# A one-core decoder step in split float32: where weights and x start in SBUF, the order of the last stores, and the place of the low-rank products

## The chip, the cores and the metric

The kernel runs on one core of one Trainium2 chip. The metric is the device time of one execution, in microseconds; the median of several runs is compared. The profile is one execution taken by the hardware profiler.

## The reference

One inference step of a decoder layer for two groups of tokens, 256 prompt tokens and 32 sample tokens (8 sequences of 4), with a width of 2048:

```python
def trunk(x, ...):
    x = x + 0.5 * rmsnorm(swiglu(rmsnorm(x, g[0]), ffn1_w_in, ffn1_w_out), g[1])
    m, sg, sh = hybrid_mixer(rmsnorm(x, g[2]), mix_w_in, gla_w_gate_up, ..., mix_w_out, s_gla, s_hgrn)
    x = x + rmsnorm(m, g[3])
    x = x + 0.5 * rmsnorm(swiglu(rmsnorm(x, g[4]), ffn2_w_in, ffn2_w_out), g[5])
    return x, sg, sh

def swiglu(x, w_in, w_out):                 # w_in 2048 x 11264, w_out 5632 x 2048
    gate, up = jnp.split(x @ w_in, 2, axis=-1)
    return (jax.nn.silu(gate) * up) @ w_out

def hybrid_mixer(h, w_in, ...):
    q, k, v, a_lr, r, hq, hf, hi, hg = jnp.split(h @ w_in, ...)
    log_alpha = jax.nn.log_sigmoid(a_lr @ gla_w_up + gla_b) / 16.0    # a_lr has 16 columns
    ...   # two gated linear recurrences (4 GLA heads, 8 HGRN2 heads), norm per head, gates
    return merged @ w_out, s_gla_new, s_hgrn_new
```

All tensors are float32, and the outputs are y for both groups and the new states.

## The kernel before

**Tiles.** All 288 tokens (T) are the columns of every product. x is held as 16 tiles of 128 x 288, one for each 128 of the 2048 features (k = 0 to 15). Each float32 operand of a large product is split into a high part (float32r) and a low part (the rest): xh[k] and xl[k] for x, hh and hl for the hidden layer, wh and wl for weights. A product is then three TensorE instructions: wh with xh (L591), wh with xl (L592), wl with xh (L593), all into one accumulator. The weights are the stationary operand (128 x 128), x the moving one (128 x 288).

**Weights.** `Weights` streams them in 672 units of 128 x 1024: two k steps of 512 columns each. SyncE's queue loads a unit into one of three `raw` buffers (L64), `pieces` splits it: ScalarE copies raw to wh (L96), VectorE subtracts to get wl (L97). There are four buffers of wh and wl, and near the borders between layers a wider pool (`begin_extra`) holds two more for some units. `ahead` keeps the split in front of TensorE.

**Blocks.** `block` makes 512 output columns: four accumulators (f = 0 to 3), for every k the four column blocks with three products each, so 12 products a k step; the last unit of a block goes by f first (`tail`), so that accumulators finish one after another. After each k, `tick(k)` emits other work. The order of instructions on each engine is made by a scheduler from the program and from `issue_after`.

**Order of the work.** Feed-forward 1: 11 chunks of gate and up blocks (16 k steps each) and output blocks (four k steps, eight at the end); the mixer; feed-forward 2 likewise. In the mixer, block v0 carries in its ticks the row mean of x (`tick1`, with `rstd` at k = 11 that gives rt), `scale_lr` at k = 8 and `a_lr` at k = 12. `a_lr` makes the 16 low-rank columns (L1445), adds up four partial sums (L1447, L1449), multiplies by rt (L1450) and splits the result and the weights for the decay product zp (L1463). The block after v0 is qk1.

**The end.** In the last output block each finished tile y[k] is added (L755), squared (L422 or L420) and scaled to z (L764); TensorE turns the last four to token order (L730, L737). `finish` makes the mean over features (L432, L160, L437: rc) and then adds z times rc to x (L809), eight prompt pieces of 128 x 512 and one sample piece zS, each followed by its store on SyncE's queue (L822, four stores L815 for zS).

**Addresses.** As the allocator places them, the bytes at which operands start in a partition, modulo 256, are: x tiles (1152 bytes each) 64 for even k and 192 for odd k; wh and wl 192 throughout (units of 4096 bytes, column blocks of 512), except for 28 units in the wider pool at 224; hidden tiles 0 and 128 in turn.

Of the kernel before, what the change touches and what calls it, by code (L numbers as in the profile page):

```python
# [30 lines left out]

RAW_BUFS = 3
HL_BUFS = 4
SCAN_LAG = 4
X_EARLY = 12


class Weights:
# [46 lines left out]
    def pieces(self, n):  # L85

        i = self.split
        raw = self.raws.pop(i)
        pool = self.extra if i in self.extra_units else self.hlp
        h = pool.tile([P, 1024], F32R, name=f"wh{i}", tag="wh")  # L90
        l = pool.tile([P, 1024], F32R, name=f"wl{i}", tag="wl")
        self.parts[i] = (h, l)
        self.split += 1
        for c in range(0, 1024, 1024 // n):
            c = slice(c, c + 1024 // n)
            i1 = self.nc.scalar.activation(h[:, c], raw[:, c], AF.Copy).ins  # L96
            i2 = self.nc.vector.tensor_tensor(l[:, c], raw[:, c], h[:, c].bitcast(F32), op=ALU.subtract).ins  # L97
            self.recent = i1, i2
            yield i1, i2

# [26 lines left out]
def trunk_kernel(ctx, tc, x_prompt, x_sample, state_gla, state_hgrn, norm_gains, f1_in, f1_out, f2_in, f2_out,  # L127
# [378 lines left out]
    class Fill:  # L506
# [3 lines left out]
        def __init__(self, pool, name, gains, gnext, some, ahead):  # L510
            self.gnext, self.name, self.some, self.ahead = gnext, name, some, ahead

            self.gains = pool.tile([P, EARLY], F32, name=f"{name}g")
            V.tensor_tensor(self.gains, gains[:, 0:EARLY], prm[:, gnext * KT:gnext * KT + EARLY], op=ALU.mult)
            self.tiles = [[[pool.tile([P, T], F32R, name=f"{name}{n}{p}{k}") for p in "hl"] for k in range(EARLY)]
                          for n in "xy"]

        def old(self):
            for k in range(EARLY):
# [62 lines left out]
    def block(name, nk, rhs, evac, width=512, tick=None, tail=1, hold=False, most=99, fill=None, late=0):  # L582

        nf, per = width // P, 1024 // width
        nu = nk // per
        ps = [mmtile(f"{name}_{f}") for f in range(nf)]
        ws = [W.next() for _ in range(EARLY // per)] if fill else []

        def mm3(dst, w, f, k, parts, start, stop):
            c = (k % per) * width + f * P  # L590
            yield lambda: PE.matmul(dst, w[0][:, c:c + P], parts[0], start=start, stop=False)  # L591
            yield lambda: PE.matmul(dst, w[0][:, c:c + P], parts[1], start=False, stop=False)  # L592
            yield lambda: PE.matmul(dst, w[1][:, c:c + P], parts[0], start=False, stop=stop)  # L593
# [48 lines left out]
    def ffn(tag, gcol, gnext, pn, before, fill=None):  # L642
# [3 lines left out]
        with ExitStack() as pools:  # L646
# [93 lines left out]
            def do_out(c, n):  # L740
# [8 lines left out]
                for o in range(4):  # L749
                    def ev(f, ps):  # L750
                        k = 4 * o + f
                        if c == 0:
                            S.activation(y[k], ps, AF.Copy)
                        else:
                            V.tensor_tensor(y[k], ps, y[k], op=ALU.add)  # L755
                        if end:
                            sq = sq_add(y[k], k, 0, KT - 2, KT - 1)
                            if k >= KT - 1:
                                lasts.append(sq)
                            if not final:  # L760
                                border[0].fill.new(k)
                            else:
# [20 lines left out]
            if final:  # L783
                zt, xt = final_tiles[0:2]

                def rest():
                    by_token(zs[2], KT - 2, *zt)
                    by_token(zs[3], KT - 1, *zt)
                    samples(zs, zt[1])

                finish(lasts[0][0], rest, zt, xt)
                return None
        return post_norm(gcol, gnext, lasts, f"post{tag}", border[0].fill), border[0]

    def finish(last, rest, zt, xt):

        (zT, zS), (xT, xS) = zt, xt
        ms = auxtile("postf")
        rc, _ = mean_cols(ms, [[sq[:, t * P:(t + 1) * P] for t in range(2)] for sq in (acc, last)], 0, 2, True)
        four = []  # L800
        for sq in (acc, last):
            r = sqp.tile([P, 4, TS], F32, name="sq4", tag="pn")
            G.tensor_copy(r, sq[:, TP:T].unsqueeze(1).broadcast_to([P, 4, TS]))
            four.append([r.rearrange("p a b -> p (a b)")])
        rest()
        rcs, _ = mean_cols(ms, four, 2, 3, False)

        def add(o, z, x, t):
            V.scalar_tensor_tensor(o, z, rc[:, t:t + 1] if t < 2 else rcs, x, op0=ALU.mult, op1=ALU.add)  # L809

        for s in range(4):
            if s == 3:
                add(zS, zS, xS, 2)
                for q in range(4):
                    nc.sync.dma_start(y_sample[:, :, q * 512:(q + 1) * 512].rearrange("b t c -> (b t) c"),  # L815
                                      zS[q * TS:(q + 1) * TS, :])

            o = (hlp if s else rawp).tile([P, 2, 512], F32, name=f"o{s}", tag="wh" if s else "raw")
            for t in range(2):
                k = slice(4 * s, 4 * s + 4)  # L820
                add(o[:, t].rearrange("p (k c) -> p k c", c=P), zT[:, k, t], xT[:, k, t], t)
                nc.sync.dma_start(y_prompt[0, t * P:(t + 1) * P, s * 512:(s + 1) * 512], o[:, t])  # L822


    def mixer(pn, border):
        with ExitStack() as mx:
# [614 lines left out]
            def a_lr():  # L1441
# [46 lines left out]
            for g in range(2):  # L1488
# [155 lines left out]
```

## Time and profile before

| | before |
|---|---|
| median of 3 runs (lowest to highest) | 2248.1 us (2247.73 to 2248.68) |
| the profiled execution: time, span | 2247.12 us, 2245.3 us |
| granted TensorE clock | 0.998 |
| TensorE, weight loads | 2233.0 us busy (99%), 2218.3 us |
| VectorE, ScalarE, GpSimd | 1386.3 us (62%), 1022.8 us (46%), 171.2 us (8%) |
| loads from memory | 167 GB/s over the span |

PE is TensorE's matmul, PEld its weight load, DVE VectorE, ACT ScalarE, POOL GpSimd, SP SyncE, and a q behind the name is the queue of an engine. A timeline row gives start and duration in us, engine, line, operation and tiles (output, then inputs), shape and count; in brackets the idle time before it. A group's row gives line, engine, operation, tiles, shapes and count, then busy us and the mean ns of one, then the idle time of the engine before it and who ended it. Rows of a window give, for each engine, the busy us and the number of instructions in the order PE, PEld, DVE, ACT, POOL, then the granted clock, the share of the DMA engines and GB/s.

### The profile page before, as it was taken

How to read it: one execution, taken by the hardware profiler on the slowest of the kernel's cores; microseconds unless marked ns; L12 is line 12 of the kernel's file. 1: busy time of each engine (PE TensorE's matmuls, PEld its weight loads, DVE VectorE, ACT ScalarE, POOL GpSimd, SP SyncE). 2: the span in 40 equal slices, each digit the busy share in tenths (PEclk: the TensorE clock that was granted, in tenths of full speed). 3: DMA queues.
4: the chain of work that ended last, by engine and by line, in shares of the span. 5: the costliest groups of instructions: out<-in, count | busy, mean ns of one | idle time of the engine just before them, and what ended most of it. 6: DMA issues, size and time to landing. Idle time of an engine off the chain costs nothing.

```text
span 2245.3 us, 43325 instructions
## 1 busy us (share of the span) xinstructions
PE 2233.0 (99%) x17832; PEld 2218.3 (99%) x17832; DVE 1386.3 (62%) x2252; ACT 1022.8 (46%) x1556; POOL 171.2 (8%) x311
## 2 busy tenths in 40 slices
PE   9999999999999999999999999999999999999998
PEld 9999999999999999999999999999999999999998
DVE  7545545554555568888888755944555465545646
ACT  6443333333334345555676654544333333333344
POOL 2000000000000001333000000530000000000005
PEclk9999999999999999999999999999999999999999
DMA  7555555555555554667565554665555555555555
GB/s 223 171 169 162 167 168 162 168 167 163 169 165 182 170 164 141 194 197 213 174 172 169 178 184 130 195 186 164 165 169 164 165 169 164 165 169 163 166 166 152
DMA packets 226758, 384.28 MB, mean 171 GB/s; under 512 B 21106, under 2 KB 60544, under 8 KB 226560
## 3 DMA queue, kind: packets, MB, share of 16 engines
q1 hardware_dynamic: 213968, 365.15, 51.8%
q0 software_dynamic: 10416, 16.18, 2.7%
q8 instruction: 140, 2.29, 0.4%
q10 hardware_dynamic: 2176, 0.18, 0.1%
q14 instruction: 58, 0.48, 0.1%
HBM read 363.75 MB, written 11.80 MB: 167 GB/s over the span
## 4 chain that ended last, share of the span: by engine, by line
PE 99%; DVE 0%; POOL 0%; ACT 0%; issue 0%; DVEq 0%; POOLq 0%
PE gate L591 10%; PE gate L593 10%; PE gate L592 10%; PE out L592 8%; PE up L593 8%; PE up L591 8%; PE up L592 8%; PE out L593 8%; PE out L591 8%; PE hfq L591 2%; PE hfq L593 2%; PE hfq L592 2%; PE mo L593 2%; PE mo L591 2%; PE mo L592 2%; PE hi L591 1%
## 5 line engine op out<-in xcount | busy, mean ns | idle before, releaser
L97 DVE TENSOR_TENSOR wl<-raw,wh 128x1024 fp32r<-128x1024 f32 (+1 forms) x676 | 821.8, 1217 | 616.7 <-ACT wh L96 612.8
L96 ACT ACTIVATE wh<-raw 128x1024 fp32r<-128x1024 f32 (+1 forms) x676 | 711.5, 1054 | 1018.8 <-PE gate L592 308.8
L591 PE MATMUL gate<-xh,wh 128*128 128x288 f32 x1660 | 489.4, 296 | 0.0
L593 PE MATMUL gate<-xh,wl 128*128 128x288 f32 x1660 | 487.7, 295 | 0.0
L592 PE MATMUL gate<-xl,wh 128*128 128x288 f32 x1660 | 485.7, 295 | 0.0
L592 PE MATMUL out<-hl,wh 128*128 128x288 f32 x1408 | 416.1, 296 | 0.0
L593 PE MATMUL up<-xh,wl 128*128 128x288 f32 x1408 | 415.6, 295 | 0.0
L593 PE MATMUL out<-hh,wl 128*128 128x288 f32 x1408 | 415.3, 295 | 0.0
L592 PE MATMUL up<-xl,wh 128*128 128x288 f32 x1408 | 415.1, 295 | 0.0
L591 PE MATMUL up<-xh,wh 128*128 128x288 f32 x1408 | 415.0, 295 | 0.0
L591 PE MATMUL out<-hh,wh 128*128 128x288 f32 x1408 | 414.1, 294 | 0.0
L591 PEld LDWEIGHTS gate<-xh,wh 128*128 128x128 f32 x1660 | 311.3, 188 | 0.9 <-DVE z L1533 0.2
L593 PEld LDWEIGHTS gate<-xh,wl 128*128 128x128 f32 x1660 | 311.4, 188 | 0.2 <-DVE wl L97 0.2
L592 PEld LDWEIGHTS gate<-xl,wh 128*128 128x128 f32 x1660 | 310.7, 188 | 0.3
L593 PEld LDWEIGHTS out<-hh,wl 128*128 128x128 f32 x1408 | 265.0, 188 | 0.0
L591 PEld LDWEIGHTS out<-hh,wh 128*128 128x128 f32 x1408 | 264.9, 188 | 0.0
L592 PEld LDWEIGHTS out<-hl,wh 128*128 128x128 f32 x1408 | 264.7, 188 | 0.0
L593 PEld LDWEIGHTS up<-xh,wl 128*128 128x128 f32 x1408 | 264.6, 188 | 0.0
L592 PEld LDWEIGHTS up<-xl,wh 128*128 128x128 f32 x1408 | 264.4, 188 | 0.0
L591 PEld LDWEIGHTS up<-xh,wh 128*128 128x128 f32 x1408 | 264.3, 188 | 0.0
L755 DVE TENSOR_TENSOR y<-out,y 128x288 f32<-128x288 f32 x288 | 121.3, 453 | 101.3 <-PE out L593 98.3
L720 POOL DMA_DIRECT2D zT<-b x40 | 23.2, 586 | 721.7 <-issue 721.7
(396 smaller groups left out, 2573.2 us busy)
## 6 DMA issues: line engine op xcount, KB each, us to landing
raw<-in_ffn_w_in_dram SPq DMA_DIRECT2D x350, 512.0 KB, 3.5
raw<-in_ffn_w_out_dram SPq DMA_DIRECT2D x176, 512.0 KB, 3.6
raw<-in_mix_w_in_dram SPq DMA_DIRECT2D x64, 512.0 KB, 4.0
raw<-in_mix_w_in_dram SPq DMA_DIRECT2D x96, 256.0 KB, 3.2
raw<-in_mix_w_out_dram SPq DMA_DIRECT2D x32, 512.0 KB, 3.7
out_dram<-s POOLq DMA_DIRECT2D x32, 256.0 KB, 2.8
s<-in_state_gla_dram SPq DMA_DIRECT2D x16, 256.0 KB, 4.7
s<-in_state_hgrn_dram SPq DMA_DIRECT2D x16, 256.0 KB, 5.3
```

Source lines behind the costliest of these rows:

```text
L96: i1 = self.nc.scalar.activation(h[:, c], raw[:, c], AF.Copy).ins
L97: i2 = self.nc.vector.tensor_tensor(l[:, c], raw[:, c], h[:, c].bitcast(F32), op=ALU.subtract).ins
L591: yield lambda: PE.matmul(dst, w[0][:, c:c + P], parts[0], start=start, stop=False)
L592: yield lambda: PE.matmul(dst, w[0][:, c:c + P], parts[1], start=False, stop=False)
L593: yield lambda: PE.matmul(dst, w[1][:, c:c + P], parts[0], start=False, stop=stop)
L720: queues[n % len(queues)].dma_start(dst[q * TS:(q + 1) * TS, 4 * g:4 * g + 4, :, cols].rearrange("p k t c -> p (k t) c"), b32[rows, q])
L755: V.tensor_tensor(y[k], ps, y[k], op=ALU.add)
```

## The change

Three edits. (1) A weight unit is [2, 544] instead of [1024], that is, its second k step starts 2176 bytes behind the first, and each buffer is 4352 bytes; a 32-column tile `cols`, a 40-column tile ahead of the wider pool and the order of the border's tiles shift what lies behind. As the allocator places them, the starts modulo 256 are then 64 for even and 192 for odd k of every unit, x as before. (2) In `finish`, the last tile is added and squared by halves of its tokens, each half has a mean and a square root of its own, and the sample's mean and the last tiles' turning come behind; the prompt pieces 0 to 2 go first for the first 128 tokens, then for the second (the scheduler mixes the two somewhat); the sample's four stores go to ScalarE's queue, and the two last prompt pieces come behind the sample's add. (3) `a_lr` ends after the partial sums and runs at k = 10; what needs rt is in `lr_parts`, at k = 12.

Distance is the start of the weights for the next product less the start of the operand that streams, modulo 256. Of the 16,034 pairs of successive large products have, in the built programs:

| distance | 0 | 64 | 128 | 192 | 32, 96, 160, 224 |
|---|---|---|---|---|---|
| before | 5664 | 1992 | 5671 | 1992 | 715 |
| after | 10482 | 842 | 1330 | 3380 | 0 |

```diff
+HALF = 512 + 32
...
-        h = pool.tile([P, 1024], F32R, name=f"wh{i}", tag="wh")
-        l = pool.tile([P, 1024], F32R, name=f"wl{i}", tag="wl")
+        h = pool.tile([P, 2, HALF], F32R, name=f"wh{i}", tag="wh")
+        l = pool.tile([P, 2, HALF], F32R, name=f"wl{i}", tag="wl")
...
-            i1 = self.nc.scalar.activation(h[:, c], raw[:, c], AF.Copy).ins
-            i2 = self.nc.vector.tensor_tensor(l[:, c], raw[:, c], h[:, c].bitcast(F32), op=ALU.subtract).ins
+            i1 = self.nc.scalar.activation(h[:, a, c], raw[:, a, c], AF.Copy).ins
+            i2 = self.nc.vector.tensor_tensor(l[:, a, c], raw[:, a, c], h[:, a, c].bitcast(F32), op=ALU.subtract).ins
...
+    cols = xpool.tile([P, 32], F32, name="cols")
...
-            c = (k % per) * width + f * P
-            yield lambda: PE.matmul(dst, w[0][:, c:c + P], parts[0], start=start, stop=False)
+            a, c = k % per, slice(f * P, f * P + P)
+            yield lambda: PE.matmul(dst, w[0][:, a, c], parts[0], start=start, stop=False)
...
+                        elif final and end and k == KT - 1:
+                            sq = sqp.tile([P, T], F32, name="sq", tag="sq")
+                            with ExitStack() as es:
+                                for r in (slice(0, P), slice(P, T)):
+                                    V.tensor_tensor(y[k][:, r], ps[:, r], y[k][:, r], op=ALU.add)
+                                    ins = V.tensor_tensor(sq[:, r], y[k][:, r], y[k][:, r], op=ALU.mult).ins
+                                    es.enter_context(tc.issue_after(ins))
+                            lasts.append((sq, None))
...
+        mss = [mmtile(f"postf{t}") for t in range(2)]
+        rc = [cols[:, 8 * t:8 * t + 1] for t in range(3)]
...
+        for sq in (acc, last):
+            for t in range(2):
+                total(sq[:, t * P:(t + 1) * P], t, sq is acc, sq is last)
+        scale(0)
+        scale(1)
...
+        for i in range(2):
+            tot = total(four[i], 2, False, i == 1)
+        behind = scale(2)
+        rest(behind, tot)
...
+        for t in range(2):
+            for s in range(3):
+                prompt(s, t)
+        add(zS, zS, xS, 2)
+        for q in range(4):
+            S.dma_start(y_sample[:, :, q * 512:(q + 1) * 512].rearrange("b t c -> (b t) c"), zS[q * TS:(q + 1) * TS, :])
+        for t in range(2):
+            prompt(3, t)
...
+            def lr_parts():
                 V.tensor_tensor(alr32[0:16, :], alr32[0:16, :], rt[0:16, :], op=ALU.mult)
...
-                          tick=lambda k: (pn.tick1(k), scale_lr() if k == 8 else a_lr() if k == 12 else None))
+                          tick=lambda k: (pn.tick1(k), scale_lr() if k == 8 else a_lr() if k == 10 else lr_parts() if k == 12 else None))
...
+            top = self.pools.enter_context(tc.tile_pool(name=f"top{gnext}", bufs=1, side="right"))
+            top.tile([P, 40], F32, name=f"gap{gnext}")
```

More of the change, by code (lines that the diff above doesn't have):

```diff
@@ L511, in __init__ @@
             self.gnext, self.name, self.some, self.ahead = gnext, name, some, ahead
-            self.gains = pool.tile([P, EARLY], F32, name=f"{name}g")
+            tiles = [[[pool.tile([P, T], F32R, name=f"{name}{n}{p}{k}") for k in range(EARLY)] for p in "hl"] for n in "xy"]
+            self.tiles = [list(zip(*hl)) for hl in tiles]
+            self.gains = pool.tile([P, 64], F32, name=f"{name}g")[:, 0:EARLY]
             V.tensor_tensor(self.gains, gains[:, 0:EARLY], prm[:, gnext * KT:gnext * KT + EARLY], op=ALU.mult)
-            self.tiles = [[[pool.tile([P, T], F32R, name=f"{name}{n}{p}{k}") for p in "hl"] for k in range(EARLY)]
-                          for n in "xy"]
         def old(self):
@@ L753, in ev @@
                             S.activation(y[k], ps, AF.Copy)
+                        elif final and end and k == KT - 1:
[6 more added lines that the diff above has]
+                            lasts.append((sq, None))
                         else:
                             V.tensor_tensor(y[k], ps, y[k], op=ALU.add)
-                        if end:
+                        if end and not (final and k == KT - 1):
                             sq = sq_add(y[k], k, 0, KT - 2, KT - 1)
@@ L759, in ev @@
                                 lasts.append(sq)
+                        if end:
                             if not final:
                                 border[0].fill.new(k)
-                            else:
+                            elif k < KT - 1:
                                 z = fp.tile([P, T], F32, name="z", tag="z", bufs=4)
@@ L784, in ffn, with rest @@
                 zt, xt = final_tiles[0:2]
-                def rest():
-                    by_token(zs[2], KT - 2, *zt)
+                def rest(ins, tot):
+                    with tc.issue_after(tot):
+                        for i in (1, 2):
+                            by_token(zs[i], KT - 4 + i, *zt)
+                    z = fp.tile([P, T], F32, name="z", tag="z", bufs=4)
+                    with tc.issue_after(ins):
+                        S.activation(z, y[KT - 1], AF.Copy, scale=gcol(KT - 1))
+                    zs.append(z)
                     by_token(zs[3], KT - 1, *zt)
@@ L797, in finish, with total, scale @@
         (zT, zS), (xT, xS) = zt, xt
-        ms = auxtile("postf")
-        rc, _ = mean_cols(ms, [[sq[:, t * P:(t + 1) * P] for t in range(2)] for sq in (acc, last)], 0, 2, True)
+        mss = [mmtile(f"postf{t}") for t in range(2)]
+        rc = [cols[:, 8 * t:8 * t + 1] for t in range(3)]
+        def total(cols, t, start, stop):
+            return PE.matmul(mss[t % 2][:, t:t + 1], cols, onesD[:, 0:1], start=start, stop=stop, skip_group_check=True).ins
+        def scale(t):
+            ins = act(rc[t], mss[t % 2][:, t:t + 1], AF.Sqrt, bias=epst)
+            V.reciprocal(rc[t], rc[t])
+            return ins
+        for sq in (acc, last):
[3 more added lines that the diff above has]
+        scale(1)
         four = []
@@ L803, in finish, with prompt @@
             G.tensor_copy(r, sq[:, TP:T].unsqueeze(1).broadcast_to([P, 4, TS]))
-            four.append([r.rearrange("p a b -> p (a b)")])
-        rest()
-        rcs, _ = mean_cols(ms, four, 2, 3, False)
-        def add(o, z, x, t):
[L809 to L822, printed above, removed]
+            four.append(r.rearrange("p a b -> p (a b)"))
+        for i in range(2):
+            tot = total(four[i], 2, False, i == 1)
+        behind = scale(2)
+        rest(behind, tot)
+        def add(o, z, x, t):
+            V.scalar_tensor_tensor(o, z, rc[t], x, op0=ALU.mult, op1=ALU.add)
+        outs = [(hlp if s else rawp).tile([P, 2, 512], F32, name=f"o{s}", tag="wh" if s else "raw") for s in range(4)]
+        def prompt(s, t):
+            k, o = slice(4 * s, 4 * s + 4), outs[s][:, t]
+            add(o.rearrange("p (k c) -> p k c", c=P), zT[:, k, t], xT[:, k, t], t)
+            nc.sync.dma_start(y_prompt[0, t * P:(t + 1) * P, s * 512:(s + 1) * 512], o)
+        for t in range(2):
[6 more added lines that the diff above has]
+            prompt(3, t)
     def mixer(pn, border):
```

11 lines of the change are left out of this document (7 added, 4 removed).

## The prediction

> **What bounds the kernel now.** I read the page first (busy times, then the chain that ended last), then TensorE's own rows in order of time, then the last 14 us of every engine, and last the neighbourhood of the low-rank products.
>
> ```profile
> span 2245.3 us, 43325 instructions
> ...
> PE 2233.0 (99%) x17832; PEld 2218.3 (99%) x17832; DVE 1386.3 (62%) x2252; ACT 1022.8 (46%) x1556; POOL 171.2 (8%) x311
> ...
> PE 99%; DVE 0%; POOL 0%; ACT 0%; issue 0%; DVEq 0%; POOLq 0%
> ```
>
> TensorE is busy for all but 12.3 us of the span, and the chain of waits is TensorE for 99%. So only two things can move the time: the pitch at which TensorE starts one product after another, and the stretch after the last product. "Busy" does not tell the pitch, because a product's row lasts 0.29 us while the next one starts 0.13 us later. The starts do. One k step is 12 products (four column blocks of three products), all with the same x tile k, xh or xl. These are the first rows of three successive steps, k = 0, 1 and 2, of the gate block of chunk 3 of the first feed-forward:
>
> ```profile
> 214.00 0.30 PE L591 MATMUL gate<-xh,wh 128*128 128x288 f32 x1
> ...
> 215.60 0.29 PE L591 MATMUL gate<-xh,wh 128*128 128x288 f32 x1
> ...
> 217.18 0.30 PE L591 MATMUL gate<-xh,wh 128*128 128x288 f32 x1
> ```
>
> Step 0 takes 1.60 us, step 1 takes 1.58 us. The same instructions and shapes, and no wait in either. The alternation goes on through the block. What differs is the address: x starts at 64 for even k and at 192 for odd k (modulo 256), the weights at 192 for both. Call distance the start of the weights being loaded for the next product less the start of the operand now streaming, modulo 256: it is 128 in the slow steps and 0 in the fast ones. Is it the address or the parity of k? The kernel has its own control. 28 of the 672 weight units lie in the wider pool, at 224. There k even has distance 160 and k odd has 32. Steps 8 and 9 of a gate block that uses such a unit, with the start of step 10:
>
> ```profile
> 761.02 0.30 PE L591 MATMUL gate<-xh,wh 128*128 128x288 f32 x1
> ...
> 762.60 0.30 PE L591 MATMUL gate<-xh,wh 128*128 128x288 f32 x1
> ...
> 764.20 0.29 PE L591 MATMUL gate<-xh,wh 128*128 128x288 f32 x1
> ```
>
> Now the even step takes 1.58 and the odd one 1.60: the parity is turned round by the address alone. The hidden tiles of the output products lie at 0 and 128; their two steps have distances 192 and 64:
>
> ```profile
> 271.27 0.29 PE L591 MATMUL out<-hh,wh 128*128 128x288 f32 x1
> ...
> 272.85 0.29 PE L591 MATMUL out<-hh,wh 128*128 128x288 f32 x1
> ...
> 274.45 0.30 PE L591 MATMUL out<-hh,wh 128*128 128x288 f32 x1
> ```
>
> 1.58 at 192, 1.60 at 64. So distances 0, 160 and 192 are fast, 32, 64 and 128 slow, by about 20 ns in a step.
>
> **The change, the layout.** It gives the two halves of a weight unit starts 128 apart, so that x of either parity meets weights at distance 0, and the hidden tiles meet distance 192. Of the 16,034 pairs of successive products 5,664 have distance 0 before and 10,482 after; 192 goes from 1,992 to 3,380; 128 falls from 5,671 to 1,330, which are the hand-overs from one k to the next, once in 12. A hand-over at 128 costs 20 ns / 12 = 1.7 ns more than one at 0.
>
> Steps that stream x in the ordinary order: 496 units of two steps, less the last unit of each of 62 blocks (their order is by column block), some 866 steps. Before they cost (1.60 + 1.58)/2 = 1.590 us, after 1.580 + 0.002 = 1.582: 8 ns x 866 = 6.9 us. Output products of the feed-forwards: 176 units, 82 of them last units, so 188 ordinary steps, 1.590 to 1.582 as well: 1.5 us. In the last units of blocks k changes after every third product, so that one pair in three has distance 128 (or 64) where it was every second; I count nothing for them. That is 8.4 us. The starts are printed to 10 ns; the same sum over all 16,034 pairs of the trace (the quoted rows are nine of them), grouped by distance modulo 512 and weighted with the counts after, gives 7.1. I take **7.7 us** off, midway, with 3.5 (only the half that is seen today, below) and 10.5 (all steps at the best of the trace, the last units too) as ends.
>
> A page speaks against this. The Trainium skill, "SBUF — State Buffer", section "Who interferes with whom", gives TensorE two independent read ports, one for the moving operand and one for the weights, and states that "PE and ACT never wait on anyone"; by that the layout is worth nothing. The rows above do not agree: 1.58 and 1.60 us for the same step, by address.
>
> The splits (L96, L97) now write two runs of 512 with a gap. Strided shapes of the same engine bound that:
>
> ```profile
> L424 DVE TENSOR_TENSOR acc<-acc,sq 128x288 f32<-128x288 f32 x87 | 39.3, 452 | 7.6 <-ACT sq L420 4.8
> ```
> ```profile
> L1104 DVE TENSOR_TENSOR Q<-Q,F 128x256 f32<-128x256 f32 x30 | 12.7, 422 | 4.4 <-PE sc L1044 4.0 <-ACT R L1119 0.3
> ```
>
> L424 is flat; the 256 elements of L1104 lie in pieces such as 2 x 32 x 4. 288 against 256 elements differ by 30 ns, 0.94 ns an element, so the strides cost nothing that shows. Zero, and at most one more fixed part of 452 - 288 x 0.94 = 181 ns a split, which the idle time of VectorE hides (second fence of the rivals). The x tiles, loads and number of splits stay.
>
> **The end.** VectorE's rows after the last product, and the last stores on SyncE's queue:
>
> ```profile
> 2231.97 0.46 DVE L755 TENSOR_TENSOR y<-out,y 128x288 f32<-128x288 f32 x1 [0.36 <-PE out L593]
> 2232.46 0.46 DVE L422 TENSOR_TENSOR sq<-y 128x288 f32<-128x288 f32 x1
> 2233.91 0.17 DVE L437 RECIPROCAL rc<-rc 128x2 f32<-128x2 f32 x1 [0.99 <-ACT rc L160]
> 2234.11 2.74 DVE L809 SCALAR_TENSOR_TENSOR o<-zT,rc,xT 128x512 f32<-128x512 f32 x4
> 2236.77 0.16 DVE L437 RECIPROCAL rc<-rc 128x1 f32<-128x1 f32 x1
> 2236.84 1.40 DVE L809 SCALAR_TENSOR_TENSOR o<-zT,rc,xT 128x512 f32<-128x512 f32 x2
> 2238.15 0.75 DVE L809 SCALAR_TENSOR_TENSOR zS<-zS,rc,xS 128x512 f32<-128x512 f32 x1
> 2238.81 1.41 DVE L809 SCALAR_TENSOR_TENSOR o<-zT,rc,xT 128x512 f32<-128x512 f32 x2
> ```
> ```profile
> 2238.93 2.12 SPq L815 DMA_DIRECT2D out_dram<-zS  x4
> 2241.14 0.88 SPq L822 DMA_DIRECT2D out_dram<-o  x2
> ```
>
> Before: from the first row to the first add of the output is 2.14 us; nine adds and a reciprocal take until 2240.22. The last two stores stand behind the sample's four on one queue, so the last goes at 2241.14 + 0.44 = 2241.6, 1.4 us after its data. After: a first half of 128 tokens takes 0.30 instead of 0.46 in each of the two operations (452 less 160 x 0.94), so its total can start 0.3 earlier; the transposes of the tile before no longer stand ahead of the totals on TensorE, nor the scaling of the last tile ahead of the square root on ScalarE. I let the adds start 0.5 us earlier and add 0.07 for the third reciprocal (pitch from 2236.77 to 2236.84). They end at 2239.8, and the last prompt store goes at once: 1.8 us sooner than 2241.6. The sample's add ends after seven adds and two reciprocals, at 2233.6 + 7 x 0.685 + 0.14 = 2238.55 (0.685 is 2.74/4). Its four stores now follow on ScalarE's queue:
>
> ```profile
> L865 ACTq DMA_DIRECT2D araw<-in_mix_w_in_dram x1: 398/398/398, 60.4 to 60.4; - x1
> ```
> ```profile
> L815 SPq DMA_DIRECT2D out_dram<-zS x4: 314/326/359, 2238.9 to 2240.7; - x4
> ```
>
> An issue there took 398 ns against 326 on SyncE, so four take 2.12 + 4 x 0.07 = 2.4 us and the last starts near 2240.4: still 1.2 us sooner than 2241.6. ScalarE has nothing left to do behind them. I take the end **1.5 us** shorter, between 0.4 (the stores on ScalarE's queue issue at half the rate) and 2.2. ScalarE's own work (three square roots first, then z, three copies of zT and zS) is done before the seventh add.
>
> **Low-rank products two steps up.** TensorE does the same work in another order:
>
> ```profile
> 901.10 2.13 PE L1445 MATMUL a_lr<-x,y 128*16 128x288 f32 x32
> ```
> ```profile
> 902.21 0.46 DVE L471 SCALAR_TENSOR_TENSOR rt<-rsls,rslsg 128x288 f32<-128x288 f32 x1
> ```
> ```profile
> 908.68 1.19 DVE L979 TENSOR_TENSOR y<-v,rt 128x288 f32<-128x288 f32 x3
> ```
> ```profile
> 909.19 0.40 PE L591 MATMUL qk<-xh,wh 128*128 128x288 f32 x1 [0.18 <-DVE y L979]
> ```
>
> Before, the three sums of the low-rank result stand between rt and the evictions of v on VectorE, and TensorE idles 0.18 us at 909.19 waiting for one of those evictions. After, the sums come before rt, but the 2.13 us of products now stand ahead of the row-mean products of pre2, so rt comes some 2 us later, and the evictions of v and the decay's products that need it with it. Against that stand the sums that no longer delay the evictions and, in the built order, eight products of qk1_0 (about 1 us) that TensorE does before it needs the first of them. I take 0, between -0.2 (the small wait gone) and +1.0.
>
> **Sum.** 7.7 + 1.5 + 0 = 9.2 us. The profiled execution took 2247.12 us with a span of 2245.3; it becomes 2237.9. The median of the runs is 1.0 us above it, 2248.1: **2238.9 us**.
>
> **Rivals.**
>
> Half of the layout only. The pairs seen today have weights at 192 (or 224). If weights at 64, which half of the steps now use, run like the average of today, half of the 7.7 us comes: 2242.8. For: no row has weights at 64. Against: at 224 the relation moved with the address, it did not vanish. Chance 0.12.
>
> No layout effect. If the pitch follows something that goes with the buffers and not with the distance, the sum is the end alone: 2246.6. Against it stand the fast even steps at 761.02. This is where the page's two ports would lead too. Chance 0.10.
>
> The low-rank order makes rt late. The late rt holds the evictions of v, qk1's accumulators and then zp; if all 2.13 us reach TensorE, they come back: 2241.0. Chance 0.05.
>
> Slower: the split with a gap binds VectorE in the mixer.
>
> ```profile
> 945.00:1262.00 317.00, 317.00 (x3250) 306.70 (x3249) 265.87 (x590) 202.71 (x455) 52.94 (x84) 1.00 0.63 185
> ```
> ```profile
> L97 DVE TENSOR_TENSOR wl<-raw,wh 128x1024 fp32r<-128x1024 f32 x78 | 95.2, 1221 | 16.2 <-ACT wh L96 14.3 <-PE tp_k L926 1.0 <-PE hms L1346 0.3
> ```
>
> VectorE has 317 - 265.9 = 51.1 us idle there over 78 splits, 0.66 us each, so it decides from a split of 1.88 us instead of 1.22. If each run of 512 cost as much as a whole row does (2.44), 78 x 1.22 - 51 = 44 us would come on top: 2283. Against it stands L1104. Chance 0.04.
>
> **How the numbers follow.** The forecast holds 0.69, with a range of its own from 2235.5 (10.5 + 2.2) to 2242.8. A comparison of this kernel tells 0.2%, 4.5 us, from no change. Faster by more: forecast, the half (2242.8 is 5.3 us off), the late rt: 0.85, a little of each falling short. Same: 0.11. Slower: 0.04. The range runs from 2234.8, just below the forecast's own low end, to 2244.5, past the half.
>
> **What would show it.** Right: even and odd steps of a gate block both at 1.58 us; the last store about 1.5 us nearer to the last product; L97 still near 1.22 us. Wrong: an alternation of 1.58 and 1.60 that remains, or moves to the other parity; a wait of qk over 1 us near 909; ScalarE's stores as the last to land.

## The result and the profile after

The changed kernel takes **2237.2 us** (median of six runs, 2236.34 to 2238.57) against 2248.1 us: 11.0 us or 0.5% faster, ratio 0.9952, 95% interval [0.9939, 0.9965]. The prediction was 2238.9 us, with a range from 2234.8 to 2244.5. The profiled execution took 2238.57 us, the longest of the six, with a span of 2236.7 us.

The page of the changed kernel, in the lines that answer to those of before:

```profile
span 2236.7 us, 43325 instructions
...
PE 2223.8 (99%) x17832; PEld 2207.8 (99%) x17832; DVE 1385.8 (62%) x2255; ACT 1021.9 (46%) x1557; POOL 169.5 (8%) x311
...
DVE 0%; DVEq 0%
```

The same number of products, and TensorE still busy for all but 12.9 us. The chain is no help this time: it ends at an add behind the last product and does not reach TensorE. The pitch must again be read from the starts. TensorE's timeline of the changed kernel, the first rows of steps k = 0 to 3 of the same gate block as in the prediction (chunk 3 of the first feed-forward):

```profile
213.57 0.29 PE L596 MATMUL gate<-xh,wh 128*128 128x288 f32 x1
...
215.15 0.29 PE L596 MATMUL gate<-xh,wh 128*128 128x288 f32 x1
...
216.72 0.29 PE L596 MATMUL gate<-xh,wh 128*128 128x288 f32 x1
...
218.30 0.30 PE L596 MATMUL gate<-xh,wh 128*128 128x288 f32 x1
```

1.58, 1.57, 1.58: the alternation of 1.60 and 1.58 is gone. But the up block that follows, with the same x at the same distance 0, runs otherwise (the first rows of its steps 0 to 2):

```profile
238.82 0.29 PE L596 MATMUL up<-xh,wh 128*128 128x288 f32 x1
...
240.41 0.30 PE L596 MATMUL up<-xh,wh 128*128 128x288 f32 x1
...
242.00 0.29 PE L596 MATMUL up<-xh,wh 128*128 128x288 f32 x1
```

1.59 in each step, even and odd. It stays so to the end of that block. So distance 0 gives not one pitch but two, 1.577 or 1.590 us a step, and a feed-forward block keeps the one it has to its end. Call them the fast and the slow phase. Over half of all x steps run in the slow one.

Last units, which I had counted at nothing, became faster too. An output block's last unit, from its first product to the first of the next block, in the kernel before (its first row, at 274.45, stands in the prediction) and in the changed one:

```profile
277.62 0.29 PE L591 MATMUL out<-hh,wh 128*128 128x288 f32 x1
```
```profile
273.73 0.29 PE L596 MATMUL out<-hh,wh 128*128 128x288 f32 x1
...
276.87 0.29 PE L596 MATMUL out<-hh,wh 128*128 128x288 f32 x1
```

3.17 us for 24 products before, 3.14 us after.

The same sum over the starts of all large products, leaving out pairs that start over 145 ns apart (waits), gives the mean pitch in ns. "x" and "hidden" name the streamed operand. The lower three rows are experiments, told below.

| kernel | x, ordinary (10,120 pairs) | x, last units (1,555) | hidden, ordinary (2,255) | hidden, last units (1,965) |
|---|---|---|---|---|
| before | 132.50 | 133.24 | 132.51 | 132.22 |
| after (x at distance 0) | 132.00 | 132.59 | 131.51 | 130.80 |
| x at 128 | 133.10 | 132.25 | 131.60 | 130.74 |
| x at 160 | 131.49 | 131.34 | 131.45 | 130.79 |
| x at 192 | 131.50 | 130.90 | 131.41 | 130.80 |

Before to after: 0.50 x 10,120 = 5.1 us, 0.65 x 1,555 = 1.0, 1.00 x 2,255 = 2.3, 1.42 x 1,965 = 2.8; together 11.2 us. The end became 0.7 us shorter. Against that, waits of TensorE between large products, counted above an ordinary pitch, went from 9.5 to 12.3 us in these two executions, and the first large product starts 0.5 us later (6.86 instead of 6.38 us into the span): -11.2 - 0.7 + 2.8 + 0.5 = -8.6, the difference of the two spans (2245.3 to 2236.7). The medians differ by 11.0, because the profiled execution of before lies 1.0 us below its median and that of after 1.4 above.

**The end.** Rows of the changed kernel from the last product on: the first half of the last tile, the first and the last adds of the output, and the stores on the two queues.

```profile
2223.68 0.30 PE L598 MATMUL out<-hh,wl 128*128 128x288 f32 x1
2224.02 0.29 DVE L763 TENSOR_TENSOR y<-out,y 128x128 f32<-128x128 f32 x1 [0.37 <-PE out L598]
...
2225.60 0.75 DVE L845 SCALAR_TENSOR_TENSOR o<-zT,cols,xT 128x512 f32<-128x512 f32 x1
...
2226.38 5.80 SPq L852 DMA_DIRECT2D out_dram<-o  x8
...
2230.41 1.41 DVE L845 SCALAR_TENSOR_TENSOR o<-zT,cols,xT 128x512 f32<-128x512 f32 x2
2230.53 1.90 ACTq L859 DMA_DIRECT2D out_dram<-zS  x4
```

The adds begin 1.58 us after the first row of the last tile (2224.02 to 2225.60) instead of 2.14. The last store goes at 2232.05, 8.0 us after that row, instead of 9.6. Yet the span ends 13.03 us after the last product's start, against 13.70. What SyncE's queue waited for last, before and after:

```profile
SPq L1640 <- DMA out_dram<-o: 1.9, 1, 1.9
```
```profile
SPq L1683 <- DMA out_dram<-zS: 2.8, 1, 2.8
```

It issued 1.6 us sooner and then waited 0.9 us longer, for ScalarE's stores, which are now the last to land. Why, the DMA engines tell. Windows of the last stretch, where the last two columns are the share of the 16 DMA engines and GB/s; before and after:

```profile
2238.00:2239.50 1.50, 0.00 (x0) 0.00 (x0) 1.50 (x4) 0.00 (x0) 0.00 (x0) 0.56 1.03 384
2239.50:2241.00 1.50, 0.00 (x0) 0.00 (x0) 0.72 (x2) 0.00 (x0) 0.00 (x0) 0.50 0.65 197
2241.00:2242.50 1.50, 0.00 (x0) 0.00 (x0) 0.00 (x0) 0.00 (x0) 0.00 (x0) 0.50 0.68 205
2242.50:2244.00 1.50, 0.00 (x0) 0.00 (x0) 0.00 (x0) 0.00 (x0) 0.00 (x0) 0.50 0.62 232
```
```profile
2228.50:2230.00 1.50, 0.00 (x0) 0.00 (x0) 1.50 (x4) 0.00 (x0) 0.00 (x0) 0.67 1.02 381
2230.00:2231.50 1.50, 0.00 (x0) 0.00 (x0) 1.50 (x3) 0.00 (x0) 0.00 (x0) 0.50 0.99 376
2231.50:2233.00 1.50, 0.00 (x0) 0.00 (x0) 0.32 (x1) 0.00 (x0) 0.00 (x0) 0.50 0.82 209
2233.00:2234.50 1.50, 0.00 (x0) 0.00 (x0) 0.00 (x0) 0.00 (x0) 0.00 (x0) 0.50 0.89 314
```

Before, the sample's four small stores, issued one by one on one queue, left a third of the DMA engines' time unused for 4.5 us. After, the engines are busy for 0.8 to 1.0 of the time until the last byte. The packets of the twelve stores take 6.75 us of all 16 engines, in both kernels. So most of the sooner issue turns into waiting: the last store goes 1.6 us sooner, but the last landing comes only 1.0 us sooner (11.33 instead of 12.35 us after the last product's start), and 0.6 us of that were there at the first landing (4.84 instead of 5.43), since the adds begin sooner.

### The profile page after: what moved, and what is told of

The parts are those of the page before. It is cut to its first block, busy times and chain, and to the rows that moved or that the text cites. A ratio compares the mean times of both kernels' runs of the same rounds, so it can differ in the third digit from the quotient of the medians.

```text
span 2236.7 us, 43325 instructions
## 1 busy us (share of the span) xinstructions
PE 2223.8 (99%) x17832; PEld 2207.8 (99%) x17832; DVE 1385.8 (62%) x2255; ACT 1021.9 (46%) x1557; POOL 169.5 (8%) x311
## 5 line engine op out<-in xcount | busy, mean ns | idle before, releaser
L101 DVE TENSOR_TENSOR wl<-raw,wh 128x1024 fp32r<-128x1024 f32 (+1 forms) x676 | 821.9, 1217 | 612.1 <-ACT wh L100 609.2
```

The source lines that it names most:

```text
L101: i2 = self.nc.vector.tensor_tensor(l[:, a, c], raw[:, a, c], h[:, a, c].bitcast(F32), op=ALU.subtract).ins
```

## The experiments

**The layout alone, the end alone, and the change without the low-rank move.** The first has the new units, the regrouped tile sets, the gap and the small tile ahead of the weights; the end and the low-rank step stay as before. The second has only the new end:

```diff
-                nc.sync.dma_start(y_sample[:, :, q * 512:(q + 1) * 512].rearrange("b t c -> (b t) c"),
...
+            S.dma_start(y_sample[:, :, q * 512:(q + 1) * 512].rearrange("b t c -> (b t) c"), zS[q * TS:(q + 1) * TS, :])
...   # with the halves of the last tile, totals and scales as in the change; units stay P x 1024
```

The third takes this back out of the changed kernel:

```diff
-                          tick=lambda k: (pn.tick1(k), scale_lr() if k == 8 else a_lr() if k == 10 else lr_parts() if k == 12 else None))
+                          tick=lambda k: (pn.tick1(k), scale_lr() if k == 8 else a_lr() if k == 12 else None))
```

> Only the layout of the change (halves of the units 128 bytes apart, tile sets regrouped, the gap below the border pools); end and low-rank order as before. Theory, the start of the weights less the start of the moving operand, modulo 256, sets the pitch: -9 to -12 us against the kernel before, 2236 to 2239 us, the mean pitch of undisturbed products from 132.54 to about 131.85 ns. Rival, the gain of the whole change came from the end and the order of the low-rank products: within 1 us of 2248.

Measured: 2237.87 us against 2248.28, ratio 0.9952 [0.994, 0.9965]; mean pitch 131.84 ns (132.54 in the kernel before). The layout is nearly the whole gain, 10.4 of 11.0 us, and every engine's instructions stand in the order of the kernel before: only addresses and the shape of the splits differ.

> Only the new end, with the small tile of its columns, which moves the weights by 128 bytes, so that x of even k now meets weights at distance 0 and x of odd k at 128 (before: the other way round), in equal numbers. Theory of the distance: the mean pitch stays at 132.5 ns, even steps take 1.58 and odd ones 1.60 us; the end alone gives -0.5 to -1.5 us, 2246.6 to 2247.6 us, since the stores land later when all are issued close together. Rival, the end is worth 2 us or more, because its stores also leave out a wait: under 2246.2. Rival on the pitch, parity of k or the buffers decide and not the distance: odd steps stay the fast ones.

Measured: 2247.65 us against 2248.28, ratio 0.9995 [0.9987, 1.0004]: 0.6 us, not told apart from nothing by the times. From the last product's start to the end the profile has 13.00 us instead of 13.70; the nine profiled kernels with this end have 12.93 to 13.15, the two with the old one 13.70 and 13.74. This kernel also turns the parity round, since its small tile moves the weights from 192 to 64. Steps k = 2 and 3 of the same gate block, and the start of k = 4:

```profile
218.34 0.29 PE L592 MATMUL gate<-xh,wh 128*128 128x288 f32 x1
...
219.92 0.30 PE L592 MATMUL gate<-xh,wh 128*128 128x288 f32 x1
...
221.52 0.29 PE L592 MATMUL gate<-xh,wh 128*128 128x288 f32 x1
```

Now the even step takes 1.58 and the odd one 1.60, over the whole kernel 1.580 and 1.602 as medians: the address turns it, not the parity of k. The mean stays at 132.52 ns, as expected.

> The changed kernel with the low-rank products put back to step 12 (layout and end as changed). Theory, the small waits of 0.5 to 1.1 us that are new in the changed kernel come from rt being late: 1 to 3 us faster than the changed kernel, 2234.5 to 2236.5, with the wait of qk back at about 0.5 us and the one of 1.14 us near 1439 gone. Rival, those waits come from the faster products, which leave VectorE and the loads less time: within 0.5 us of the changed kernel's 2237.2, with the waits still there.

Measured: 2237.33 us, 0.15 us from the changed kernel. My theory of a late rt fell: the move is worth nothing that shows, and the new small waits do not come from it. The row that TensorE waits for at the start of the second feed-forward's chunk 1, in the changed kernel and in this one:

```profile
1440.17 0.40 PE L596 MATMUL gate<-xh,wh 128*128 128x288 f32 x1 [0.85 <-DVE u L679]
```
```profile
1438.99 0.40 PE L596 MATMUL gate<-xh,wh 128*128 128x288 f32 x1 [0.49 <-DVE u L679]
```

It is there without the move. The rival's time came true, but its reason, faster products, is not shown: the kernel with the end alone, whose products are no faster, has this wait too (0.80 us), and the layout alone, whose products are as fast as these, has none. Where it comes from stays open. At the low-rank products two small waits changed places, with the move and without it:

```profile
905.93 0.40 PE L596 MATMUL qk<-xh,wh 128*128 128x288 f32 x1 [0.40 <-DVE y L1018]
...
910.44 0.51 PE L1504 MATMUL zp<-alr,ahl 96*128 96x288 f32 x2
```
```profile
904.83 0.40 PE L596 MATMUL qk<-xh,wh 128*128 128x288 f32 x1 [0.22 <-DVE y L1018]
...
907.77 0.50 PE L1502 MATMUL zp<-alr,ahl 96*128 96x288 f32 x2 [0.17 <-POOL qm L941]
```

With the move qk waits 0.18 us longer, and the decay product zp no longer waits its 0.17.

**Other distances.** The small tile ahead of the weights and the gap below the border pools, made larger, move all weights against x; the hidden tiles move with the weights and keep distance 192. The order of instructions on every engine is that of the changed kernel. To 192:

```diff
-    cols = xpool.tile([P, 32], F32, name="cols")
+    cols = xpool.tile([P, 80], F32, name="cols")
...
-            top.tile([P, 40], F32, name=f"gap{gnext}")
+            top.tile([P, 56], F32, name=f"gap{gnext}")
```

> The changed kernel with 192 bytes more ahead of the weights (and the border pools moved to match): x now meets its weights at distance 192 in both parities, as the hidden tiles do, whose distance stays at 192. Theory, distance 192 is the better place, since output steps keep 1.576 to 1.580 us there while x at distance 0 has whole blocks at 1.590: all x steps near 1.578, 4 to 8 us faster than the changed kernel, 2229 to 2233. Rival, blocks at 1.590 come from something other than the distance (order of the column blocks, the block before, loads): within 1.5 us of 2237.2.

Measured: **2229.74 us** (2229.5 to 2230.04), ratio to before 0.9917 [0.9903, 0.993], 7.4 us faster than the changed kernel. The up block that ran at 1.59 before, steps 0 to 3:

```profile
238.20 0.29 PE L596 MATMUL up<-xh,wh 128*128 128x288 f32 x1
...
239.78 0.29 PE L596 MATMUL up<-xh,wh 128*128 128x288 f32 x1
...
241.35 0.29 PE L596 MATMUL up<-xh,wh 128*128 128x288 f32 x1
...
242.93 0.29 PE L596 MATMUL up<-xh,wh 128*128 128x288 f32 x1
```

1.58, 1.57, 1.58. By the table, the ordinary and last-unit pitches come to 7.9 us less than after: the whole gain.

To 128, with tiles of 64 and 72 instead of 80 and 56:

> The changed kernel with 128 bytes more ahead of the weights (border pools moved to match): x now meets its weights at distance 128 in both parities; all else as in the changed kernel, the hidden tiles still at 192. Theory, the distance decides and not the evenness of the two halves: x steps of 1.60 us in both parities, against a mean of 1.588 now, so (133.4 - 132.0) ns x 10,115 = 14 us above the changed kernel, about 2251, slower than even the kernel before. Rival, what helped was that both parities got the same distance, whichever: within 2 us of 2237.2.

Measured: 2246.72 us, ratio to before 0.9994 [0.9985, 1.0003]. The same up block, steps 0 to 2:

```profile
240.15 0.29 PE L596 MATMUL up<-xh,wh 128*128 128x288 f32 x1
...
241.75 0.29 PE L596 MATMUL up<-xh,wh 128*128 128x288 f32 x1
...
243.34 0.29 PE L596 MATMUL up<-xh,wh 128*128 128x288 f32 x1
```

1.60 and 1.59 (1.597 as the median of all): equal for both parities, and slow. The rival, that evenness was what helped, falls. I was 4 us too high: steps at 128 next to each other cost 1.597 and not 1.602, and the last units, whose hand-overs are now at 0, cost 132.25 and not 132.6. Two kernels with the same instructions in the same order, 64 bytes apart in the distance of weights and x, differ by 17.0 us.

The place of the weights by itself is not what counts. In the built programs they start at 64 and 192 here as in the changed kernel, with the parities changed over. The hidden products, whose weights move by the same bytes while their distance stays, keep an ordinary pitch of 131.4 to 131.6 ns in all four lower rows of the table. That the period is 256 bytes, the kernel before bears out: tiles k and k + 2 of x start 2304 bytes apart, which is 256 modulo 512, and as medians their ordinary steps take 1.601 and 1.602 us at distance 128, 1.576 and 1.581 at 0.

The Trainium skill, "SBUF — State Buffer", section "Who interferes with whom", gives TensorE two independent read ports and lets it never wait on anyone, by which both would be equal; these runs do not agree with it.

To 160, with tiles of 72 and 64:

> The changed kernel with x at distance 160 in both parities, the hidden tiles still at 192. Theory, the good stretch of distances takes in 160, since the steps of the kernel before with units at 224 took 1.58 us at 160: near the kernel with x at 192, 2229 to 2232, x steps 1.577 to 1.583. Rival, 192 alone is clean, and 160 locks in a slower phase as 0 does: 2236 to 2242.

Measured: 2230.66 us, ratio to before 0.9923 [0.9912, 0.9935], ordinary x pitch 131.49 ns. The good stretch takes in 160; no slow phase shows (1.575 us as the median of even steps, 1.579 of odd ones).

**What sets the slow phase at distance 0.** In the changed kernel blocks of the first feed-forward right behind an output block run at 1.577 us a step and the up blocks, each behind a gate block, at 1.590. A gate block's last unit takes k inside and the column block outside. The experiment turns that for 43 blocks:

```diff
+        rows = rhs is xrhs and tick is None and not fill and not hold and tail == 1
+        for k in range((nu - tail) * per, nk) if rows else ():
+            for f in range(nf):
+                mm(ws[0], f, k)
         for f in range(nf):
-            for k in range((nu - tail) * per, nk):
+            for k in range((nu - tail) * per, nk) if not rows else ():
```

> The changed kernel (x at distance 0) with the last unit of 43 gate, up, mixer and other x blocks in the ordinary order, both k outside and the column blocks inside, and the four evictions behind it. Theory: at distance 0 the steps run at 1.577 or 1.590 us by whole blocks, and what throws a block into the slower phase is the last unit of the block before, where k changes after every third product: ordinary x pairs fall from 132.0 to about 131.5 ns and the kernel gains up to 5 us, less what the bunched evictions cost. Rival, the phase is set elsewhere (the block's own start, the accumulators): blocks at 1.590 remain, 2237 or more.

Measured: 2235.72 us, 1.5 us faster than the changed kernel. The up block's steps 0 to 2:

```profile
238.34 0.30 PE L596 MATMUL up<-xh,wh 128*128 128x288 f32 x1
...
239.91 0.30 PE L596 MATMUL up<-xh,wh 128*128 128x288 f32 x1
...
241.49 0.30 PE L596 MATMUL up<-xh,wh 128*128 128x288 f32 x1
```

1.57 and 1.58: the block that follows such a last unit now keeps the fast phase. So do 19 of the 20 up blocks behind a turned last unit; in the changed kernel all 20 ran at 1.590. The median of all x steps is 1.577 us (1.589 after), the mean ordinary pitch 131.64 instead of 132.00 ns. But the up block that is left, chunk 1 of the second feed-forward, has such a last unit before it as well and stays slow; the first rows of its steps 0 to 2:

```profile
1462.10 0.29 PE L596 MATMUL up<-xh,wh 128*128 128x288 f32 x1
...
1463.69 0.30 PE L596 MATMUL up<-xh,wh 128*128 128x288 f32 x1
...
1465.29 0.29 PE L596 MATMUL up<-xh,wh 128*128 128x288 f32 x1
```

The gate block ahead of it ran in the slow phase already, and three blocks of the mixer behind turned last units, each behind a slow block, stay at 1.590 too. Read together: a last unit in the ordinary order hands on the phase of its block, and one in the other order can change it, from fast to slow for the up blocks. In one place of the changed kernel it goes the other way: the gate block of chunk 1 of the first feed-forward is fast behind a slow up block; its first products stand in another order. So theory and rival both held in part, and what else chooses the phase is open; the distance at the change of k, once in 12 pairs, is 128 at distance 0, 64 at 192 and 32 at 160, and no run varies it alone. The pitches fell by 4.4 us in the two profiled executions, and waits rose by 1.0: the four evictions now stand behind one another at the end of a block, and pairs that start over 145 ns apart rise from 106 to 139. The medians differ by only 1.5 us, since the two profiled executions lie 1.4 above and 0.8 below them.

**The order by column for most units, at distance 192.** Last units start products every 130.8 to 130.9 ns there and ordinary ones every 131.4 to 131.5.

```diff
+                elif tick is None and not fill and not late:
+                    for f in range(nf) if k == u * per else ():
+                        for j in range(k, k + per):
+                            mm(w, f, j)
```

> The kernel with x at 192, and in blocks without ticks, fill or late x the ordinary units in the order of the last units (column block outside, the unit's two k inside): some 400 units of 24 products. Theory, the order itself is faster at these distances, because last units start a product every 130.8 to 130.9 ns and ordinary ones every 131.4 to 131.5: 400 x 24 x 0.6 ns = 5.8 us faster than 2229.7, about 2224. Rival, the last units are faster through what stands behind them (the next block, an accumulator change) and not through the order: 2229.7 within 1 us.

Measured: **2226.88 us** as the median (five runs from 2226.3 to 2227.5, one of 2239.7), 2.9 us less than x at 192 (2.4 less than the same program in the run `sample_earlier` below): half of what I expected, ratio to before 0.9914 [0.9898, 0.993]. Taken over ordinary and last units, x came down from 131.42 to 131.22 ns, 2.3 us for 11,672 pairs. The hidden products stayed at 131.1: what their ordinary units gained (131.41 to 131.11) their last units lost (130.80 to 131.11). So the theory holds in part for x, and for hidden products the rival does: their last units lost their advantage when all units were alike, as if it lay in the change of order between units; no run tests that by itself. It is the fastest version found, 21 us under the kernel before.

**The end.** The first try moved the sample's add in the text only:

> The kernel with x at 192, with the sample's add and its four stores two adds earlier, as the fifth (its scale and its transposes are there by then); the prompt's last two adds and stores still end the queue at the same time. Theory, the end brought 0.7 and not 1.5 us because the last stores of both queues are issued together and land 2.5 to 3.0 us later: now the last prompt stores land alone, in about 2.3 us, and the end is 0.4 to 0.7 us shorter than 12.96 us from the last product's start. Rival, the 64 KB of each prompt store alone set the landing, or the wait behind them does: 12.96 within 0.15 us.

Measured: 2229.32 us, 13.09 us from the last product to the end. The scheduler still put the add seventh, and every engine's order is that of the kernel with x at 192; so this run tells nothing of its reason, only that two kernels with the same instructions agree to 0.4 us in time and 0.13 us in the end. The second try holds the later adds behind it:

```diff
+        sample = add(zS, zS, xS, 2)
...
+        with tc.issue_after(sample):
+            for s in (1, 2):
+                prompt(s, 1)
+            for t in range(2):
+                prompt(3, t)
```

> The kernel with x at 192, with the four adds after the sample's held behind it, so that the sample's add is the fifth in fact and not only in the text. Theory of the bunched landing: the four stores on ScalarE's queue go about 1.3 us earlier and land before the prompt's last two, which then take 2.3 and not 2.5 to 3.0 us; the end from the last product's start 12.4 to 12.6 instead of 12.96 us. Rival, the landing of the last prompt store takes 3 us with or without company: 12.96 within 0.15.

Measured: 2230.37 us and 13.42 us: longer, against both expectations. The prompt's last store goes alone, 8.17 us after the last product's start, and needs 3.55 us to land. (Each store of the prompt has 256 KB, not 64 as the expectation of the first try says; the sample's have 64.) Windows of its end:

```profile
2222.50:2224.00 1.50, 0.00 (x0) 0.00 (x0) 0.97 (x2) 0.00 (x0) 0.00 (x0) 0.50 0.92 306
2224.00:2225.50 1.50, 0.00 (x0) 0.00 (x0) 0.00 (x0) 0.00 (x0) 0.00 (x0) 0.50 1.02 369
```

The DMA engines are full here too. The last four prompt stores now go 0.66 us apart, and one alone takes 0.71 us at the 369 GB/s of the second row, the sample's stores coming on top. By this estimate landing is set by the bytes in front, not by when the small stores go. The bunching theory falls.

The third puts the sample's stores back on SyncE's queue:

```diff
-            S.dma_start(y_sample[:, :, q * 512:(q + 1) * 512].rearrange("b t c -> (b t) c"), zS[q * TS:(q + 1) * TS, :])
+            nc.sync.dma_start(y_sample[:, :, q * 512:(q + 1) * 512].rearrange("b t c -> (b t) c"), zS[q * TS:(q + 1) * TS, :])
```

> The kernel with x at 192, with the sample's four stores put back on SyncE's queue, all else of the new end kept (first half of 128 tokens, totals, order of the adds). Theory: the last store goes at 9.3 to 9.5 us after the last product's start instead of 8.4, lands in 2.4 instead of 3.0, and the end is 12.96 + 0.2 to 0.6 us: ScalarE's queue is worth less than the 1.0 us by which it issues sooner. Rival, issue alone decides: 13.9 to 14.1.

Measured: 2230.29 us and 13.29 us, in the expected band: the last store goes at 9.58 instead of 8.33 us, lands in 2.37 instead of 2.94, and the end is 0.33 us longer (two executions with the same end differed by 0.13). Windows of its end:

```profile
2222.50:2224.00 1.50, 0.00 (x0) 0.00 (x0) 0.85 (x2) 0.00 (x0) 0.00 (x0) 0.50 0.66 197
2224.00:2225.50 1.50, 0.00 (x0) 0.00 (x0) 0.00 (x0) 0.00 (x0) 0.00 (x0) 0.50 0.58 167
```

Here the engines are busy for only 0.58 to 0.66 again, as in the kernel before. The second queue is worth what it fills of that, 0.33 us, out of 1.25 us that it saves at issue. The Trainium skill, "Trainium Kernel Development and Optimization", section "Key Constraints", says that the queues of several engines share the same 16 DMA engines, and that issuing from several only saves the time of issue. The rows agree: two queues together fill 0.8 to 1.0 of the 16 engines' time and no more, and the gain is less than the time saved at issue.

## Why the prediction was right, and where its terms were off

**The mechanism** was right: the distance between the weights and the streamed operand sets the pitch, and both parities are now alike. The sign "even and odd steps at 1.58" came true in gate blocks and not in up blocks (1.59). That the total came within 1.7 us is luck in part: the layout was put 2.7 us too low and the end 0.8 too high, and within the layout the ordinary x steps were put too high and the rest too low.

**The layout's size**: 7.7 us taken, 10.4 measured by itself, at the upper end of its bounds (3.5 to 10.5). The terms of the sum erred both ways. Ordinary x steps were put at 6.9 us and brought 5.1, because I took distance 0 to be one pitch: in before, where these steps stand between slow ones, they take 1.580 us on the mean; with all steps at 0 many blocks run at 1.590, and the mean is 1.584. Ordinary output steps were put at 1.5 and brought 2.3. Last units, "counted at nothing", brought 3.8 (1.0 and 2.8). The step that failed is that one: their pairs of distance 192, which rise with the change, stood in the count of pairs, and I gave them no price.

**The end**: 1.5 us taken, 0.7 measured. The start of the adds (0.5 us earlier taken, 0.56 measured) and the last issue (1.2 us sooner taken, 1.6 measured) were right or better. The step that failed is that a store issued sooner ends as much sooner: the stores' packets take 6.75 us of the 16 DMA engines and the landing gave back 0.6 us; another 0.35 us passed behind the last landing (1.70 instead of 1.35 us to the end of the span), whose cause stays open. The sign "ScalarE's stores as the last to land", named as one of a wrong prediction, did come.

**The low-rank step**: 0 taken, nothing that shows measured (0.15 us), as a wait of qk that grew (0.40, under the 1 us named) against a small one that went, that of zp.

**The splits with a gap** cost nothing. The whole kernel's splits before and after:

```profile
L97 DVE TENSOR_TENSOR wl<-raw,wh 128x1024 fp32r<-128x1024 f32 (+1 forms) x676 | 821.8, 1217 | 616.7 <-ACT wh L96 612.8
```
```profile
L101 DVE TENSOR_TENSOR wl<-raw,wh 128x1024 fp32r<-128x1024 f32 (+1 forms) x676 | 821.9, 1217 | 612.1 <-ACT wh L100 609.2
```

1217 ns in both: the rival of 2283 us had no ground. "No layout effect" falls with the layout alone, and "half of the layout" with weights at 64 that run like those at 192 (132.00 and 132.04 ns for the two kinds in the layout alone).

**Not foreseen**: 2.8 us of new waits in the profiled execution. Those between the layout alone, the change without the low-rank move and the changed kernel vary (10.5, 10.9 and 12.3 us above the pitch), so part of it belongs to that execution; before had 9.5.

## What to carry to other kernels

Where TensorE is bound by its own pitch, list for each pair of successive products where the next weights start against the operand that is streaming, modulo 256, and group the starts by it: here a tile larger by 192 bytes was worth 7.4 us over the changed kernel. Measure several distances before one is chosen: the kernel's own hidden tiles, at 192, were a better guide than the faster half of x, at 0. Before queues are rearranged at an end, look at the share of the DMA engines there: what another queue can win is the idle share.

## What was not expected of the hardware

At distance 0 the pitch has two lasting values, 1.577 and 1.590 us for 12 products, and which one holds depends on the order of products in the unit before and on the phase of the block before; at 160 and 192 only the faster shows, at 128 1.597. At 192, last units with k inside and the column block outside run at 130.8 to 130.9 ns a product, 0.6 ns less than the ordinary units between them; with most units in that order it is 131.1 to 131.2. What in the chip makes the distance count, no run here shows.
